# A decoder layer on one core: the loads for splitting the mixer's weights wait for an operand of group 3 of the first feed-forward block, and a split takes five steps of it in place of six

## The chip, the cores and the metric

The kernel runs on one core of one Trainium2 chip. The metric is the device time of one execution in microseconds (us). Five engines work side by side, each on its own list of instructions in a fixed order: PE (TensorE, matrix products), DVE (VectorE), ACT (ScalarE), POOL (GpSimd) and SP (SyncE, which here only issues DMA transfers). ACT also issues DMA transfers, from its own list.

## The reference

One decoder layer over 1024 rows of width 1024, in float32. Cut to what matters here:

```
x <- LN1(alpha*x + 0.5*SwiGLU_1(x))      # first feed-forward block, width 2816
x <- LN2(alpha*x + mixer(x))             # mixer: proj = x @ w_in, sparse attention, gated MLP, @ w_out
x <- LN3(alpha*x + 0.5*SwiGLU_2(x))      # second feed-forward block
```

Products must be exact to almost float32. Each operand is therefore split into a high part and a remainder, and a product is three matmuls (high x high, high x low, low x high).

## The kernel before

**Splitting.** `split` (L84 to L88) makes the two parts of an operand: ACT writes the rounded high part (L87), DVE or POOL subtracts it from the operand (L88).

**The first half of a feed-forward block** (`ffn`, name f1 for the first block) goes over 11 groups, g = 0 to 10. Each group is a Winograd-like scheme of seven products m = 1 to 7; a product is 24 matmuls of 128x512 into a pair of PSUM banks (tile `ab`). Products 1 and 2 of groups 0 to 5 are done ahead, so that the program then goes through five products (6, 7, 5, 4, 3) for groups 1 to 5 and through seven (1, 6, 2, 7, 5, 4, 3) for groups 6 to 10. The weights of group g+1 (four tiles `w`, L342) are loaded while group g is worked on. `left` prepares left operands up to four products ahead: DVE forms sums of weight tiles (L288 to L293), then `parts` splits them; ACT writes `hi`, DVE or POOL writes `lo`. The results of a product are taken out of PSUM by DVE (L382, L413, L416, L423, L429 in the order of the products) and, from group 6 on, after product 1 by an ACT copy (tile `c`, L356). Gated results `h`, `u`, `c` go back to DRAM (`f<-h`, `f<-c`, `f<-u`, L445 to L450), and sums kept in DRAM come back for the next group (`u<-f_c`, `h<-f`, L434, L435).

**The second half** multiplies the stored results by the weights w2 (eleven loads of 1 MB, L504, and `hid` loads, L552; PSUM tiles `y` and `z`).

**Splitting the mixer's weights beside it.** `make_parts` (L99) is a generator that runs through 28 weight pieces: load (L117, SP), split (ACT, DVE, tiles `made`), store the two parts to DRAM (L137, issued by ACT). `product` of the first block takes a step of it after each quarter of a product. The loaded pieces use two buffers (`N_W`), which the `hid` loads use later too; the split pieces use the 15 large buffers, of which 14 hold the split right operand `xs` all through the groups. Each load also has to find its buffer free, so that load i+2 waits for the split of piece i.

**The order.** Outside an early part written in a fixed order, a scheduler places the instructions on each engine by its own model of time and dependencies; an instruction may so stand far ahead of its place in the program. On the chip each engine, and the SP list, goes through its order and waits where an instruction is not ready.

Of the kernel before, what the change touches and what calls it, by code (L numbers as in the profile page):

```python
# [7 lines left out]
F32 = mybir.dt.float32  # L8
# [5 lines left out]
ALU = mybir.AluOpType  # L14
# [17 lines left out]
N_W = PAR["NW"]  # L32
N_BIG = PAR["NB"]
EARLY = 6
class Net:
# [63 lines left out]
    def make_parts(self):  # L99

        nc, ins = self.nc, self.ins
        flat = lambda x: x.rearrange("p k c -> p (k c)")
        todo = [(("A", j), flat(ins["w_inA"][j])) for j in range(4)]
        todo += [(("T", i), flat(ins["w_inT"][i])) for i in (4, 5)]
        todo += [((n, j), flat(ins["w_in" + n][j])) for n in "BC" for j in range(4)]
        todo += [("ws", flat(ins["wsT"]))]
        todo += [(("T", i), flat(ins["w_inT"][i])) for i in range(2)]
        todo += [(("O", i), ins["w_out"][i]) for i in range(4, 8)]
        todo += [(("T", i), flat(ins["w_inT"][i])) for i in range(2, 4)]
        todo += [("wuk", flat(ins["w_ukT"]))]  # L110
        todo += [(("O", i), ins["w_out"][i]) for i in range(4)]
        raws = {}

        def load(i):
            if i < len(todo):
                raws[i] = self.raw("made", (P, todo[i][1].shape[-1]))
                nc.sync.dma_start(raws[i], todo[i][1])  # L117

        load(0)
        for i, (key, src) in enumerate(todo):  # L120
            x, n = raws[i], src.shape[-1]
            load(i + 1)
            if key == "ws":
                y = x.rearrange("p (g c) -> p g c", g=NH)
                nc.gpsimd.affine_select(
                    out=y, in_=y, pattern=[[0, NH], [1, P]], compare_op=ALU.is_ge, fill=0.0, base=0, channel_multiplier=-1
                )
            if key == "wuk":
                nc.scalar.activation(x, x, AF.Copy, scale=0.125)
            yield  # L130
            t = self.large("made", (P, 2, n))
            self.split(x, t[:, 0], t[:, 1])
            yield
            yield
            name = self.name("made")
            self.made[key] = self.dram.tile([P, 2, n], F32, tag=name, name=name)
            nc.scalar.dma_start(self.made[key], t.bitcast(F32))  # L137
            for _ in range(3):
                yield

    def load_w(self, key, s, shape=(P, 1024)):
# [115 lines left out]
    def ffn(self, name, w13, w2, begin, meanwhile, load_acc, norm, after, side=iter(())):  # L257
# [10 lines left out]
        nc, V = self.nc, self.nc.vector  # L268
# [8 lines left out]
        blocks, first_blocks, lefts, xs, sums, due, summed = {}, {}, {}, {}, {}, [], []  # L277

        def left(n):

            for g, m in plan[len(lefts) : n]:
                if g < EARLY and m in (1, 2):
                    lefts[g, m] = self.parts(first_blocks[g, m], V)
                    continue
                a = blocks[g]
                if m == 6:
                    a[5] = self.page("S", (P, 2, HALF))
                    V.tensor_tensor(a[5], a[7], a[4], ALU.add)  # L288
                    a[6] = a[1]
                    V.tensor_tensor(a[7], a[1], a[7], ALU.subtract)  # L290
                    V.tensor_tensor(a[6], a[5], a[1], ALU.subtract)  # L291
                if m == (5 if g else 3):
                    V.tensor_tensor(a[2], a[2], a[6], ALU.subtract)  # L293
                    a[3] = a[2]
                lefts[g, m] = self.parts(a[m], E(PAR["LE"][m - 1] if g > 1 else 0))

        def halves(j):

            if j == 0:
                lefts[0, 1] = tuple(self.page(n, (P, 2, HALF), F32R) for n in ("hi", "lo"))  # L300
            self.split(first_blocks[0, 1][:, j], *(x[:, j] for x in lefts[0, 1]))

        def right(n):

            for i in range(len(xs), min(n, len(xplan))):
                m, k = xplan[i]
                for q in xplan[len(summed) : i + 2 if n > 8 else i + 1]:
                    self.x_sums(*q)
                    summed.append(q)
                if k % 2 == 0:  # L310
                    self.xp = self.large("xs", (P, 2, 2, HALF))
                xs[m, k] = self.xp[:, k % 2, 0], self.xp[:, k % 2, 1]
                self.split(self.x_block(self.X_BLOCK[m])[:, k], *xs[m, k])

        def product(g, m, ps, start=True):
            now = plan.index((g, m))
            for k in range(4):
                if now >= 3:
                    right(8 + (4 * (now - 3) + k + 1) // 2)
                if k == 1:  # L320
                    for f in due:
                        f()
                    due.clear()
                if k or now > 2 * EARLY + 4:
                    left(now + (3 if now < 2 * EARLY + 5 else 1 + (k + PAR["LS"]) // 4))
                w, x = lefts[g, m], xs[m, k]
                for j in range(2):
                    ks = slice(k * P, (k + 1) * P)
                    self.mm3(ps[:, j], (w[0][:, j, ks], w[1][:, j, ks]), x, start and k == 0, k == 3, m in (1, 2, 3, 5))
                if g > 1 and now > 2 * EARLY:  # L330
                    next(side, None)

        def load(g, m, s=slice(0, 2), of=None):
# [18 lines left out]
        def first(g, a):  # L352

            product(g, 1, a)
            c1 = page("c1")
            nc.scalar.activation(c1, a, AF.Copy)  # L356
            return c1

        def first_early(g, a):

            product(g, 1, a)
            c1 = sums[g] = page("c1")

            def keep():
                nc.scalar.activation(c1, a, AF.Copy)
                if g:
                    nc.scalar.dma_start(spill[g], c1)

            due.append(keep)

        def group(g, begun=None):
# [3 lines left out]
            else:  # L375
                a = pair()
                sums[g], h1 = first(g, a), page("h1")
                h11 = h1[:, 0]
            b = pair()
            product(g, 6, b)  # L380
            u2 = sums[g]
            then(lambda b=b: V.tensor_tensor(u2, b, sums[g], ALU.add))  # L382
# [84 lines left out]
        with self.in_order():  # L467
            halves(0)
            right(1)
            halves(1)  # L470
            right(4)
            left(3)
            right(8)
            for g in range(0, EARLY, 2):
                if g == EARLY - 2:
                    for m in (7, 4, 1, 2):
                        load(0, m)
                two = [pair() for _ in range(2)]
                hh = self.raw("hh", (P, 2, HALF))
                for e in range(2):  # L480
                    first_early(g + e, two[e])
                    if g == 0:
                        meanwhile(e)
                for e in range(2):
                    product(g + e, 2, two[e], start=False)

                    def done(g=g + e, h=hh[:, e], ps=two[e]):
                        gated(h, ps)
                        nc.sync.dma_start(hid[g, :, 0], h)
                        if g == 0:  # L490
                            again[g] = None, h

                    due.append(done)
            group(0, again[0])
# [22 lines left out]
        raws, pieces, last, acc = {}, {}, {}, []  # L517
# [50 lines left out]
        for m in order2[:6]:  # L568
# [5 lines left out]
            for k in range(NG):  # L574
# [5 lines left out]
                if m == 7 and k in PAR["NK"]:  # L580
                    t = PAR["NK"].index(k)
# [659 lines left out]
```

## Time and profile before

| | before |
|---|---|
| time, median of 3 runs | 1777.25 us (1776.61 to 1777.44) |
| the profiled execution: its time | 1778.62 us |
| the profiled execution: its span, first to last instruction | 1776.9 us |
| PE busy | 1726.3 us, 97% of the span |
| DVE, ACT, POOL busy | 75%, 45%, 22% |

The first half of the first feed-forward block takes the first 446 us or so of the span, the mixer starts at about 640 us. The profiled execution is 1.37 us above the median.

### The profile page before, as it was taken

To read this page: it belongs to the slowest core of one execution; us is meant where nothing else is said; L and a number is where in the kernel's file an instruction comes from. 1 tells how busy PE (TensorE), PEld (TensorE's weight loads), DVE (VectorE), ACT (ScalarE), POOL (GpSimd) and SP (SyncE) were. 2 spreads that over 40 slices of the span, in tenths; PEclk is the share of its full clock that TensorE was granted. 3 is DMA by queue.
4 is the path that set the end of the run, shared out by engine and by line. 5 is a ranking of instruction groups with operands and counts; after the bars stand their busy time and mean duration, and the time that the engine had idled before them with its cause. 6 is when DMAs were issued, how large, how long until landed. Compare 5 with 4: busy or idle time off the path is not lost.

```text
span 1776.9 us, 22235 instructions
## 1 busy us (share of the span) xinstructions
PE 1726.3 (97%) x8016; PEld 1447.2 (81%) x8016; DVE 1330.1 (75%) x2215; ACT 792.1 (45%) x1346; POOL 396.8 (22%) x287
## 2 busy tenths in 40 slices
PE   8989999999999999999989999999999999999997
PEld 6868778888888888998877888888788888888886
DVE  5779886765895864899979877877777555589586
ACT  5423333423545515667787662452322222355551
POOL 0004242222000361001246321100423222200036
PEclk9999999999999999999999999999999999999999
DMA  7458866757545343225512007335443322754532
GB/s 285 151 222 291 300 252 262 267 203 287 188 123 184 101 163 119 96 87 170 198 36 96 1 1 238 135 119 201 142 178 123 132 89 89 286 192 127 177 101 83
DMA packets 89709, 288.64 MB, mean 162 GB/s; under 512 B 9088, under 2 KB 9600, under 8 KB 85504
## 3 DMA queue, kind: packets, MB, share of 16 engines
q1 hardware_dynamic: 82208, 252.33, 40.2%
q10 hardware_dynamic: 5472, 32.02, 4.5%
q0 software_dynamic: 1920, 2.89, 0.8%
q8 instruction: 63, 1.03, 0.2%
q14 instruction: 46, 0.38, 0.1%
HBM read 195.15 MB, written 89.16 MB: 160 GB/s over the span
## 4 chain that ended last, share of the span: by engine, by line
PE 68%; DVE 8%; ACT 4%; DMA 2%; issue 2%; POOL 1%; SPq 0%; POOLq 0%; ACTq 0%; DVEq 0%
PE ab L152 10%; PE ab L153 10%; PE ab L154 10%; PE y L152 5%; PE y L154 5%; PE y L153 5%; PE z L154 3%; PE z L152 3%; PE z L153 3%; PE pN L152 2%; ACT act L832 2%; PE pN L153 2%; PE pN L154 2%; PE tr L1010 2%; DVE dve L823 1%
## 5 line engine op out<-in xcount | busy, mean ns | idle before, releaser
L152 PE MATMUL ab<-xs,hi 128*128 128x512 f32 x1232 | 482.9, 392 | 23.1 <-DVE c L416 9.2
L153 PE MATMUL ab<-xs,hi 128*128 128x512 f32 x1232 | 481.6, 391 | 0.0
L154 PE MATMUL ab<-xs,lo 128*128 128x512 f32 x1232 | 481.2, 391 | 0.0
L152 PEld LDWEIGHTS ab<-xs,hi 128*128 128x128 f32 x1232 | 232.7, 189 | 76.5 <-issue 17.6
L153 PEld LDWEIGHTS ab<-xs,hi 128*128 128x128 f32 x1232 | 232.7, 189 | 48.5 <-DVE xs L88 0.4
L154 PEld LDWEIGHTS ab<-xs,lo 128*128 128x128 f32 x1232 | 232.7, 189 | 48.4
L88 POOL TENSOR_TENSOR lo<-w,hi 128x1024 fp32r<-128x1024 f32 x54 | 139.8, 2588 | 561.0 <-ACT hi L87 536.7
L87 ACT ACTIVATE hi<-w 128x1024 fp32r<-128x1024 f32 (+1 forms) x134 | 137.6, 1040 | 163.4 <-DVE w L291 123.5
L88 DVE TENSOR_TENSOR lo<-w,hi 128x1024 fp32r<-128x1024 f32 (+1 forms) x80 | 94.8, 1195 | 43.1 <-ACT hi L87 42.5
L88 DVE TENSOR_TENSOR a<-hid,a 128x512 fp32r<-128x512 f32 x132 | 93.5, 708 | 26.1 <-ACT a L87 26.1
L87 ACT ACTIVATE a<-hid 128x512 fp32r<-128x512 f32 x132 | 82.0, 621 | 54.5 <-DMA hid<-f 48.3
L153 PE MATMUL y<-b,a 128*128 128x512 f32 x264 | 102.7, 389 | 0.0
L154 PE MATMUL y<-b,a 128*128 128x512 f32 x264 | 102.7, 389 | 0.0
L153 PE MATMUL z<-b,a 128*128 128x512 f32 x264 | 102.7, 389 | 0.0
L154 PE MATMUL z<-b,a 128*128 128x512 f32 x264 | 102.7, 389 | 0.0
L152 PE MATMUL z<-b,a 128*128 128x512 f32 x264 | 102.5, 389 | 0.0
L152 PE MATMUL y<-b,a 128*128 128x512 f32 x264 | 102.0, 389 | 0.0
L88 DVE TENSOR_TENSOR b<-w,b 128x512 fp32r<-128x512 f32 x110 | 77.2, 702 | 33.0 <-ACT b L87 32.8
L832 ACT ACTIVATE act<-score,tk 128x768 int8<-128x768 f32 (+2 forms) x93 | 87.2, 937 | 29.7 <-DVE tk L844 21.8
L349 ACT ACTIVATE h<-c 128x512 f32<-128x512 f32 x34 | 21.4, 630 | 162.8 <-DVE c L416 115.1
L87 ACT ACTIVATE b<-w 128x512 fp32r<-128x512 f32 x110 | 68.4, 622 | 51.6 <-PE z L154 38.6
L593 POOL TENSOR_TENSOR xacc<-xacc,T 128x512 f32<-128x512 f32 x8 | 13.0, 1652 | 333.8 <-DVE T L566 166.9
(267 smaller groups left out, 3576.9 us busy)
## 6 DMA issues: line engine op xcount, KB each, us to landing
w<-in_ffn_w_dram SPq DMA_DIRECT2D x110, 512.0 KB, 6.5
hid<-f SPq DMA_DIRECT2D x60, 512.0 KB, 3.8
w<-in_ffn_w_dram SPq DMA_DIRECT2D x22, 1024.0 KB, 11.2
f<-h SPq DMA_DIRECT2D x32, 512.0 KB, 3.8
made<-made ACTq DMA_DIRECT2D x16, 1024.0 KB, 6.4
f<-c SPq DMA_DIRECT2D x22, 512.0 KB, 3.9
wo<-made SPq DMA_DIRECT2D x8, 1024.0 KB, 7.6
xr<-x_spill SPq DMA_DIRECT2D x16, 512.0 KB, 5.8
```

The source lines that it names most:

```text
L87: nc.scalar.activation(hi, src, AF.Copy)
L88: (eng or nc.vector).tensor_tensor(lo, src, hi.bitcast(F32), ALU.subtract)
L152: mm(out, a[0], b[0], start=start, stop=False, skip_group_check=skip)
L153: mm(out, a[0], b[1], start=False, stop=False, skip_group_check=skip)
L154: mm(out, a[1], b[0], start=False, stop=stop, skip_group_check=skip)
L349: nc.scalar.activation(t, c[:, 0], AF.Silu)
L593: nc.gpsimd.tensor_tensor(acc[j][:, HALF:], acc[j][:, HALF:], T[j], ALU.add)
L823: V.tensor_scalar(self.marks("dve", s.shape[-1]), s, f, None, ALU.is_lt, ALU.add, accum_out=val[:, j : j + 1])
L832: nc.scalar.activation(out, s, AF.Sign, bias=fj, scale=-1.0, accum_out=val[:, j : j + 1])
L1010: nc.tensor.transpose(pt[:, hh * P : (hh + 1) * P], ps4[hh][:, j * P : (j + 1) * P], self.ident)
```

## The change

The generator starts with group 3 in place of group 2 (`g > 2`), and it takes five steps to a piece in place of six. The first two loads are each preceded by a POOL operation that writes two columns of their buffer, from the newest high part of a left operand (`recent`); a load into that buffer then has to wait for that operation and so for that operand. In the scheduled program this is the high part of product 4 of group 3.

```
         def load(i):
             if i < len(todo):
                 raws[i] = self.raw("made", (P, todo[i][1].shape[-1]))
+                if i < N_W:
+                    t = self.recent.bitcast(F32)[:, 0, :2]
+                    nc.gpsimd.tensor_tensor(raws[i][:, :2], t, t, ALU.subtract)
                 nc.sync.dma_start(raws[i], todo[i][1])
...
             nc.scalar.dma_start(self.made[key], t.bitcast(F32))
-            for _ in range(3):
+            for _ in range(2):
                 yield
...
                 lefts[g, m] = self.parts(a[m], E(PAR["LE"][m - 1] if g > 1 else 0))
+                self.recent = lefts[g, m][0]
...
-                if g > 1 and now > 2 * EARLY:
+                if g > 2 and now > 2 * EARLY:
                     next(side, None)
```

**The list of SP at the weights of group 2.** The names are `made` for a loaded piece, `u_103` and `h_104` for the sums of group 1 that come back, `w_110` to `w_113` for the weights of group 2, `f` for what group 0 stores. Before (the first load of a piece stands one row above):

```order
L117 DMA made_1000<-in_w_inA_dram 128x768
L117 DMA made_1060<-in_w_inA_dram 128x768
L117 DMA made_1121<-in_w_inA_dram 128x768
L434 DMA u_103_783<-f_c_76 128x1024
L435 DMA h_104_784<-f_75 128x512
L445 DMA f_75<-u_88_651 128x512
L342 DMA w_110_834<-in_ffn_w_dram 128x1024
L342 DMA w_111_836<-in_ffn_w_dram 128x1024
L342 DMA w_112_838<-in_ffn_w_dram 128x1024
L449 DMA f_75<-c_89_652 128x1024
L449 DMA f_75<-h_90_653 128x1024
L342 DMA w_113_840<-in_ffn_w_dram 128x1024
```

The same place now:

```order
L346 DMA w_87_649<-in_ffn_w_dram 128x1024
L438 DMA u_103_783<-f_c_76 128x1024
L439 DMA h_104_784<-f_75 128x512
L449 DMA f_75<-u_88_651 128x512
L346 DMA w_110_834<-in_ffn_w_dram 128x1024
L346 DMA w_111_836<-in_ffn_w_dram 128x1024
L346 DMA w_112_838<-in_ffn_w_dram 128x1024
L453 DMA f_75<-c_89_652 128x1024
L453 DMA f_75<-h_90_653 128x1024
L346 DMA w_113_840<-in_ffn_w_dram 128x1024
L454 DMA f_75<-u_88_651 128x512
```

Four loads of pieces are gone from the list ahead of the weights of group 2; the first load of a piece now stands 19 rows behind `w_113`, after the weights of group 4 (`w_162` to `w_165`).

**The list of DVE in group 3.** `S` and `w` with L288 to L293 (now L291 to L296) are sums for the left operands of group 4, `ab` is a PSUM result of group 3, `made` a split. Before:

```order
L382 TENSOR_TENSOR u_165_1186<-ab_1198,u_165_1186 128x1024
L413 TENSOR_TENSOR u_175_1238<-ab_1241,u_165_1186 128x1024
L288 TENSOR_TENSOR S_1279<-w_173_1234,w_174_1236 128x1024
L290 TENSOR_TENSOR w_173_1234<-w_171_1230,w_173_1234 128x1024
L88 TENSOR_TENSOR made_1556<-made_1497,made_1556 128x836
L291 TENSOR_TENSOR w_171_1230<-S_1279,w_171_1230 128x1024
L293 TENSOR_TENSOR w_172_1232<-w_172_1232,w_171_1230 128x1024
L88 TENSOR_TENSOR lo_1284<-w_171_1230,hi_1283 128x1024
L416 TENSOR_TENSOR c_176_1239<-ab_1278,u_175_1238 128x1024
```

Now:

```order
L386 TENSOR_TENSOR u_153_1158<-ab_1170,u_153_1158 128x1024
L88 TENSOR_TENSOR made_1193<-made_1181,made_1193 128x768
L417 TENSOR_TENSOR u_166_1219<-ab_1222,u_153_1158 128x1024
L291 TENSOR_TENSOR S_1258<-w_164_1215,w_165_1217 128x1024
L293 TENSOR_TENSOR w_164_1215<-w_162_1211,w_164_1215 128x1024
L294 TENSOR_TENSOR w_162_1211<-S_1258,w_162_1211 128x1024
L296 TENSOR_TENSOR w_163_1213<-w_163_1213,w_162_1211 128x1024
L88 TENSOR_TENSOR made_1247<-made_1184,made_1247 128x768
L88 TENSOR_TENSOR lo_1263<-w_162_1211,hi_1262 128x1024
L420 TENSOR_TENSOR c_167_1220<-ab_1257,u_166_1219 128x1024
```

The first split of all now stands between the first two results of group 3, the second ahead of the third result. From the first result of a group (L382) to that of the next, DVE had three splits in groups 2 to 4; it now has none in group 2, four in group 3, two in group 4 and four in group 5.

**The list of ACT in group 6.** `c` is the copy of the first result of a group, `hi` a left operand, `h` a gate; the rows run from the copy of group 6 on. Before:

```order
L356 ACTIVATE c_271_1843<-ab_1812 128x1024
L87 ACTIVATE hi_1848<-S_1726 128x1024
L87 ACTIVATE hi_1885<-w_243_1651 128x1024
L87 ACTIVATE made_2037<-made_1974 128x1024
L137 DMA made_2059<-made_2037 128x2048
L349 ACTIVATE h_272_1845<-ab_1812 128x512
L87 ACTIVATE hi_1932<-w_241_1647 128x1024
L87 ACTIVATE made_2103<-made_2029 128x1024
```

Now:

```order
L360 ACTIVATE c_268_1838<-ab_1802 128x1024
L87 ACTIVATE hi_1843<-S_1719 128x1024
L87 ACTIVATE hi_1877<-w_237_1639 128x1024
L87 ACTIVATE made_1669<-made_1607 128x836
L140 DMA made_1690<-made_1669 128x1672
L87 ACTIVATE made_1712<-made_1661 128x836
L353 ACTIVATE h_269_1840<-ab_1802 128x512
L87 ACTIVATE hi_1927<-w_235_1635 128x1024
```

Between the copies of groups 6, 7, 8, 9 and 10 ACT had four, four, three and no splits; it now has five, four, four and five, and one more behind the copy of group 10. Eleven of the 28 splits stood behind the copy of group 6, now nineteen.

## Rows read from the trace of the kernel before

**Rows 1.** The page: the span, and busy time, share and instructions of each engine.

```profile
span 1776.9 us, 22235 instructions
PE 1726.3 (97%) x8016; PEld 1447.2 (81%) x8016; DVE 1330.1 (75%) x2215; ACT 792.1 (45%) x1346; POOL 396.8 (22%) x287
```

**Rows 2.** Stretches of the span: length, then busy time and number of instructions (x) of PE, weight loads, DVE, ACT and POOL, the granted TensorE clock as a share of 2.4 GHz, the DMA share and GB/s.

```profile
90.00:120.00 30.00, 29.08 (x128) 23.47 (x127) 25.24 (x26) 9.93 (x12) 0.00 (x0) 1.00 0.63 232
120.00:150.00 30.00, 24.04 (x98) 19.41 (x97) 23.83 (x18) 8.76 (x10) 10.87 (x4) 0.89 0.73 261
150.00:240.00 90.00, 86.09 (x378) 70.23 (x377) 80.12 (x63) 29.23 (x34) 33.84 (x13) 1.00 0.80 297
240.00:360.00 120.00, 119.38 (x526) 98.22 (x525) 84.33 (x74) 44.21 (x49) 31.27 (x12) 1.00 0.69 261
360.00:390.00 30.00, 30.00 (x134) 24.84 (x133) 19.05 (x19) 11.22 (x13) 10.14 (x4) 1.00 0.63 236
390.00:480.00 90.00, 90.00 (x398) 74.51 (x397) 65.57 (x90) 33.29 (x56) 9.99 (x5) 1.00 0.59 213
480.00:600.00 120.00, 120.00 (x531) 99.37 (x530) 88.61 (x141) 64.03 (x106) 4.87 (x4) 1.00 0.49 156
```

**Rows 3.** The matmuls of PE ahead of which it stood idle, in order of time: start, duration, line and operation, and in brackets the idle time and what ended it.

```profile
104.64 0.47 PE L152 MATMUL ab<-xs,hi 128*128 128x512 f32 x1 [0.72 <-DVE c L406]
133.10 0.77 PE L152 MATMUL ab<-xs,hi 128*128 128x512 f32 x1 [5.96 <-DVE c L416]
179.78 0.47 PE L152 MATMUL ab<-xs,hi 128*128 128x512 f32 x1 [0.96 <-DVE u L382]
...
237.76 0.47 PE L152 MATMUL ab<-xs,hi 128*128 128x512 f32 x1 [2.68 <-DVE u L382]
```

**Rows 4.** DVE, in order of time, around the wait for the weights of group 2.

```profile
111.43 0.68 DVE L442 TENSOR_TENSOR h<-hh,h 128x512 f32<-128x512 f32 x1
...
116.91 1.22 DVE L413 TENSOR_TENSOR u<-ab,u 128x1024 f32<-128x1024 f32 x1
125.68 1.23 DVE L288 TENSOR_TENSOR S<-w,w 128x1024 f32<-128x1024 f32 x1 [7.56 <-DMA w<-in_ffn_w_dram]
...
131.74 1.22 DVE L416 TENSOR_TENSOR c<-ab,u 128x1024 f32<-128x1024 f32 x1
```

**Rows 5.** The SP list, in order of time (start, time from the first to the last issue of the row), and behind it a row of its waits: who waited for whom, us in total, times, the longest.

```profile
82.17 25.02 SPq L117 DMA_DIRECT2D made<-in_w_inA_dram  x4
...
109.20 1.01 SPq L445 DMA_DIRECT2D f<-u  x1
110.25 2.13 SPq L342 DMA_DIRECT2D w<-in_ffn_w_dram  x3
...
113.42 0.33 SPq L449 DMA_DIRECT2D f<-h  x1
113.85 0.36 SPq L342 DMA_DIRECT2D w<-in_ffn_w_dram  x1
...
SPq L117 <- DVE made L88: 119.0, 24, 11.8
```

**Rows 6.** One stretch (columns as in rows 2), and the issues of weight loads up to 480 us: number, KB each, median us from issue to landing.

```profile
118.00:126.00 8.00, 8.00 (x37) 6.64 (x36) 0.44 (x2) 0.00 (x0) 0.00 (x0) 1.00 1.02 415
...
w<-in_ffn_w_dram SPq DMA_DIRECT2D x55, 512.0 KB, 7.2
```

**Rows 7.** ACT, in order of time: the split pieces at the first and the last of twelve in a row, the longest distance between two of them, and the row of its waits for their stores.

```profile
255.33 1.07 ACT L87 ACTIVATE made<-made 128x1024 fp32r<-128x1024 f32 x1 [1.89 <-DMA made<-made]
...
303.80 1.06 ACT L87 ACTIVATE made<-made 128x1024 fp32r<-128x1024 f32 x1 [2.73 <-DMA made<-made]
...
314.73 1.05 ACT L87 ACTIVATE made<-made 128x1024 fp32r<-128x1024 f32 x1
...
361.85 1.06 ACT L87 ACTIVATE made<-made 128x1024 fp32r<-128x1024 f32 x1 [1.02 <-DMA made<-made]
...
ACT made L87 <- DMA made<-made: 65.8, 20, 9.5
```

**Rows 8.** ACT: the copies of groups 6 and 10, the first and the last of five.

```profile
259.82 1.03 ACT L356 ACTIVATE c<-ab 128x1024 f32<-128x1024 f32 x1 [2.87 <-DVE c L440]
...
413.34 1.03 ACT L356 ACTIVATE c<-ab 128x1024 f32<-128x1024 f32 x1 [1.62 <-PE ab L154]
```

**Rows 9.** DVE: a split of a piece while POOL is idle, and one while POOL works.

```profile
155.20 1.02 DVE L88 TENSOR_TENSOR made<-made,made 128x836 fp32r<-128x836 f32 x1
...
221.79 3.15 DVE L88 TENSOR_TENSOR made<-made,made 128x836 fp32r<-128x836 f32 x1 [0.92 <-ACT made L87]
```

**Rows 10.** SP: the loads of the weights w2. ACT: an operand of the second half. A stretch at the end of the groups (columns as in rows 2).

```profile
369.91 0.38 SPq L504 DMA_DIRECT2D w<-in_ffn_w_dram  x1
...
416.19 19.27 SPq L504 DMA_DIRECT2D w<-in_ffn_w_dram  x8
...
447.15 0.63 ACT L87 ACTIVATE a<-hid 128x512 fp32r<-128x512 f32 x1 [2.76 <-DMA hid<-f]
...
430.00:440.00 10.00, 10.00 (x46) 8.29 (x45) 5.03 (x7) 3.58 (x7) 0.00 (x0) 1.00 1.03 410
```

**Rows 11.** POOL: its smallest tensor operations (ns, shortest, median and longest), and its waits up to 480 us.

```profile
L174 POOL TENSOR_TENSOR rstd<-rs,mhalf x26: 542/1192/2739, 603.2 to 1769.7; 128x1 f32<-128x1 f32 x24, 128x4 f32<-128x4 f32 x2
...
POOL lo L88 <- ACT hi L87: 302.8, 19, 131.9
```

More of the change, by code (lines that the diff above doesn't have):

```diff
@@ L116, in load @@
                 raws[i] = self.raw("made", (P, todo[i][1].shape[-1]))
+                if i < N_W:
+                    t = self.recent.bitcast(F32)[:, 0, :2]
+                    nc.gpsimd.tensor_tensor(raws[i][:, :2], t, t, ALU.subtract)
                 nc.sync.dma_start(raws[i], todo[i][1])
@@ L137, in make_parts @@
             nc.scalar.dma_start(self.made[key], t.bitcast(F32))
-            for _ in range(3):
+            for _ in range(2):
                 yield
@@ L295, in left @@
                 lefts[g, m] = self.parts(a[m], E(PAR["LE"][m - 1] if g > 1 else 0))
+                self.recent = lefts[g, m][0]
         def halves(j):
@@ L329, in product @@
                     self.mm3(ps[:, j], (w[0][:, j, ks], w[1][:, j, ks]), x, start and k == 0, k == 3, m in (1, 2, 3, 5))
-                if g > 1 and now > 2 * EARLY:
+                if g > 2 and now > 2 * EARLY:
                     next(side, None)
```

## The prediction

> **What bounds the kernel now.** I read the page first, then stretches of the span, then where PE waits, and then the lists of the engines there. PE is busy for 97% of the span [rows 1], so time can only be won where PE stands idle or runs slowly. The stretches show where that is [rows 2]: 30 us of full work hold 134 matmuls, 90 us hold 398 and 120 us hold 531, which is 120/531 = 0.226 us each. Against this the stretches from 90 us on are short by 134-128 = 6, 134-98 = 36, 398-378 = 20 and 531-526 = 5 matmuls, that is by 1.4, 8.1, 4.5 and 1.1 us, 15.1 us together. This is the span in which pieces of the mixer's weights are split beside the groups. From 360 us to 600 us nothing is lost.
>
> The largest loss has one cause. PE waits 5.96 us, up to 133.10, for the DVE operation L416 that takes a result of group 1 out of PSUM [rows 3]. That operation stands in DVE's list behind sums of group 2's weights, and DVE waits 7.56 us for a weight tile, to 125.68 [rows 4]. The tile is the last of group 2, w_113, issued at 113.85, so that it took 11.8 us to be there [rows 5]. The rest of the 8.1 us is the clock: its mean in that stretch is 0.89 [rows 2], so for about 0.11 x 30 / 0.5 = 6.6 us PE had the lower level, 1.2 GHz in place of 2.4, after the idle time.
>
> **Term 1: the weights of group 2.** Before, four loads of pieces hold the SP list from 82.17 for 25 us [rows 5], because each needs a buffer that an earlier split frees; behind them stand the sums of group 1 (u, h), a store and the weights. Now they are gone from that place. But the next rows of SP show that this isn't the whole wait: the store f<-u, which needs a gate from DVE, is issued only at 109.20, 2.0 us after the pieces' row ends, and w_113 follows f<-h, whose source is ready at 112.1 (L442 [rows 4]). So the load moves only as far as DVE and ACT move. Two splits on DVE fall away ahead of L442, about 1.0 us each [rows 9], and some half a us in which DVE waits for ACT's half of one (an estimate): 2.5 us, so the first issue of this batch comes at about 106.7 and w_113 at about 111. What falls away beside that is traffic. While the tile is awaited, the DMA engines are full, at 415 GB/s [rows 6], and loads and stores of pieces are among what they move. The batch that remains is 256 KB, three tiles, two stores and the last tile of 512 KB each, 3.4 MB, which at 415 GB/s takes 8.2 us: 115 at the earliest; by the median of such loads, 7.2 us [rows 6], w_113 is there at 118. From the sum at 125.68 to the next matmul at 133.10 are 7.4 us [rows 3, 4]; PE ran dry at 127.1, which the loss of 0.7 us at 104.64 [rows 3] no longer delays, so the sum must start by 127.1-0.7-7.4 = 119.0. That is 1 us to spare. I take the 8.1 and the 1.4 us as won and charge 0.5 us for a rest of the wait: -9.0. Bounds: 9.5 won, or, if the tile lands only 2.5 us earlier (123.2), 119.0-123.2 = 4.2 us of waiting stay, and with the clock (8.1 us were lost for 5.96 of waiting) 5.7 us.
>
> The Trainium skill has a rule against my figure here: "DMA: Bandwidth & Descriptors", Bandwidth, says that traffic between HBM and SBUF is held to about 358 GB/s for a core. By it the batch would take 9.5 us, the tile would land 1.3 us later, and the term would be -8.7. The row shows 415 GB/s in this very stretch, so the measurement decides.
>
> **Term 2: groups 2 to 5.** DVE is what is short there: 80.1 of 90 us busy from 150 on, and PE waits for L382, the first result of a group [rows 2, 3]. A split costs DVE 1.0 us, and up to 3.15 us while POOL works [rows 9]. Three splits to each group went with 4.5 us of loss over three group starts, 1.5 each. Now group 2 has none, group 4 two, groups 3 and 5 four. I charge the two heavy groups 1.5 each and the others nothing: 3.0 us in place of 4.5, so -1.5. Bounds: all 4.5 won, or one new wait of the old kind (below).
>
> **Term 3: groups 6 to 10.** A split piece has one large buffer, so ACT can't start the next until the last is stored: it waited 65.8 us for stores in all. From the first to the last of twelve pieces it took 361.85-255.33 = 106.5 us, eleven steps of 9.68 us [rows 7], against a group of (413.34-259.82)/4 = 38.4 us [rows 8]: four pieces, 38.7. So the chain just kept pace with PE, and the loss there was 1.1 us over three groups. Now nineteen pieces stand there, and of five, four, four and five between the copies the last has a second buffer, since the first operands of group 10 free one. That leaves 17 pieces, 16 steps from one to the next, in 4 x 38.4 = 153.5 us, less 3.1 us for the copy and two operands that stand ahead (1.03 us each), plus 4.4 us by which a copy may be late (product 6 lasts 24 x 0.226 = 5.4, the copy 1.03): 154.8 us for 16 x 9.68 = 154.9. Again it just keeps pace, and five of them are shorter (836 columns). I charge the old loss for four and a half groups in place of three, 1.7 in place of 1.1: +0.6. Bounds: -1.1 if it never binds, +20.1 in the third rival.
>
> **Terms at nothing.** The two POOL operations cost 0.5 to 2.7 us each by the smallest of POOL [rows 11]; POOL stands idle for 302.8 us waiting for operands [rows 11], and what they delay is the first load, which the order puts behind the weights of group 4 anyway. If that cover were gone, 2.4 us at the median would be added to the first load. The weights w2 lose the early start of their first load (369.91 [rows 10]): it now waits in SP behind the last pieces, to about 7 us into group 10, and three more follow the very last split. Seven more of the eight late loads took 19 us for buffers that group 10 frees, which doesn't change. The DMA engines, full at 410 GB/s there [rows 10], get some 7 MB more, 17 us of work, while ACT reaches the fifth operand of the second half only at 447 and waits for hid, not w2 [rows 10]. That is 31 us after these loads began (416.19), which leaves room for 7 us in SP's list and a part of the 17, so I add nothing.
>
> **The sum.** -9.0 -1.5 +0.6 = -9.9 us against the profiled execution: 1778.62-9.9 = 1768.7. It lay 1.37 us above the median, so the forecast is **1767.4 us**.
>
> **Rivals.**
> - *All of it goes.* No wait is left: -15.1, 1762.1. For it: half of the DVE-bound stretch has fewer splits. Against: two groups have more. Chance 0.08.
> - *The stall only moves.* In group 3 the second split now stands ahead of the third result. Load, split, store and next split must fit into the four products, 4 x 5.4 = 21.7 us, before PE needs that result out of PSUM: the first load, behind the weights of group 4, lands some 9 us into the group (an estimate: 7.2 us [rows 6] behind an issue 2 us into it), split, store and next split are a step of 9.68, and a remainder and the result, 1.2 us each [rows 4], stand behind: 21.1 us, without any room. If the store meets the weight loads it is later (the longest wait for one was 9.5 [rows 7]), and a wait like that of group 1 with its slow clock comes back: 8.1 us, net -1.8, 1775.5. Chance 0.20.
> - *The chain of splits becomes the bound* (the other side). If a step takes 10.93 us, as from 303.80 to 314.73 [rows 7], 16 take 174.9, 20.1 us more than they have; ACT is then late for the copies and PE waits: -10.5+20.1 = +9.6, 1786.9. It turns to slower than before at (154.8+10.5)/16 = 10.3 us a step; the mean was 9.68. Chance 0.11. The Trainium skill ("TensorE: Matmul & The Clock Gate", on the engines' queues) says that ACT and DVE are strictly first in, first out, so that a waiting split holds all behind it; the 65.8 us of waits agree.
> - *The change does not do what it says.* The last tile of group 2 is late from its own batch, not from the pieces: the 5.7 us of term 1's bound stay, 0.5 of which are charged already: -4.7, 1772.6. Chance 0.08.
> - *The second half starts dry.* If the chain runs 5 us late (10.0 us a step), so do the last weights w2 behind it in SP, and the room above is used up: -4.9, 1772.4. Chance 0.05.
>
> **How the numbers follow.** The forecast has 0.48. A measurement of this kernel tells about 0.2%, 3.5 us, from no change, so faster means below 1773.7 and slower above 1780.8. Faster: the forecast, the first, the fourth and the fifth case, and a little of the second, 0.72; same: most of the second and a mild third, 0.17; slower 0.11. The range goes from the first rival's 1762.0 to 1775.5, where the second ends; beyond lie half of the second and the third.
>
> **What would show it.** Right: no load of a piece on SP before about 160 us; DVE's wait for w in group 2 under 2 us; 120 to 150 us with 130 or more matmuls and a clock of 1.00; the copy of group 10 about 10 us earlier than 413.34; splits of pieces until after it, ACT's waits for stores near 65 us, and 1 to 3 us of waits for DVE in groups 3 and 5. Wrong: an idle time over 4 us with a lower clock in groups 3 to 5, a distance of over 10.3 us between pieces behind group 6, or waits for w2 or hid at the start of the second half.

## The result and the profile after

The change makes the kernel slower: 1786.82 us median of 6 runs (1784.37 to 1791.16) against 1777.98 us for the kernel before, ratio 1.0055 with a 95% interval from 1.0044 to 1.0066. The forecast was 1767.4 us, with a range that ended at 1775.5. The profiled execution of after has a span of 1782.6 us (before: 1776.9 [rows 1]).

The stretches of after, with the columns of rows 2:

```profile
90.00:120.00 30.00, 30.00 (x134) 24.83 (x133) 21.79 (x22) 6.76 (x8) 0.00 (x0) 1.00 0.39 131
120.00:150.00 30.00, 27.63 (x122) 22.58 (x121) 26.30 (x21) 7.45 (x9) 10.12 (x4) 1.00 0.41 150
150.00:240.00 90.00, 89.26 (x393) 73.44 (x392) 72.59 (x63) 29.36 (x36) 31.68 (x14) 1.00 0.71 260
240.00:360.00 120.00, 116.62 (x511) 95.30 (x511) 89.81 (x75) 44.15 (x50) 33.33 (x13) 1.00 0.68 257
360.00:390.00 30.00, 29.48 (x131) 24.11 (x130) 18.06 (x16) 11.84 (x14) 10.45 (x4) 1.00 0.66 263
390.00:480.00 90.00, 81.58 (x347) 66.73 (x348) 65.26 (x86) 31.64 (x49) 10.46 (x4) 0.94 0.78 297
480.00:600.00 120.00, 118.07 (x521) 97.44 (x521) 86.12 (x139) 68.44 (x114) 0.00 (x0) 1.00 0.50 156
```

Up to 240 us nearly all of the old loss is gone: 12 and 5 matmuls are missing where 6+36 and 20 were [rows 2]. But 20 are missing from 240 to 360 us (5 before), 51 from 390 to 480 us (none before), with a mean clock of 0.94, and 10 from 480 to 600 us (none before). The matmuls of PE ahead of which it stood idle say where:

```profile
127.69 0.47 PE L155 MATMUL ab<-xs,hi 128*128 128x512 f32 x1 [2.37 <-DVE c L420]
199.56 0.47 PE L155 MATMUL ab<-xs,hi 128*128 128x512 f32 x1 [0.74 <-DVE u L386]
265.88 0.50 PE L155 MATMUL ab<-xs,hi 128*128 128x512 f32 x1 [0.75 <-DVE h L354]
299.81 0.50 PE L155 MATMUL ab<-xs,hi 128*128 128x512 f32 x1 [0.99 <-DVE c L386]
329.24 0.47 PE L155 MATMUL ab<-xs,hi 128*128 128x512 f32 x1 [1.61 <-DVE c L433]
...
458.67 1.65 PE L155 MATMUL y<-b,a 128*128 128x512 f32 x3 [7.43 <-ACT b L87]
482.35 0.50 PE L155 MATMUL y<-b,a 128*128 128x512 f32 x1 [1.93 <-ACT T L591]
```

The wait of 5.96 us at group 2 [rows 3] has become one of 2.37, and a new one of 7.43 us stands at the start of the second half. The places in the program that can be found in both traces give the account:

| us from the start | before | after | difference | change since the place above |
|---|---|---|---|---|
| copy of group 6 (ACT) | 259.82 | 249.35 | -10.5 | -10.5 |
| first matmul of `y` (PE) | 445.8 | 440.2 | -5.6 | +4.9 |
| first result of `y` out of PSUM (ACT, `T`) | 474.39 | 481.72 | +7.3 | +12.9 |
| end of the span | 1776.9 | 1782.6 | +5.7 | -1.6 |

(The copies: after at 249.35 and 410.06, before [rows 8].) So the change wins 10.5 us in groups 1 to 5, gives 4.9 back in groups 6 to 10 and 12.9 at the start of the second half. The last 1.6 us were not followed to a place. What ACT and SP do there, after:

```profile
408.48 0.33 SPq L120 DMA_DIRECT2D made<-in_w_out_dram  x1
409.62 0.38 SPq L556 DMA_DIRECT2D hid<-f  x1
...
413.52 1.56 SPq L508 DMA_DIRECT2D w<-in_ffn_w_dram  x1
...
419.84 20.28 SPq L508 DMA_DIRECT2D w<-in_ffn_w_dram  x9
440.21 4.83 SPq L556 DMA_DIRECT2D hid<-f  x2
...
457.47 0.63 ACT L87 ACTIVATE a<-hid 128x512 fp32r<-128x512 f32 x1 [13.86 <-DMA hid<-f]
```

In before the fifth operand from `hid` was split at 447.15 [rows 10], though its load was issued only 0.6 us earlier (439.60). After, the load is issued at 440.21, and ACT stands idle for 13.86 us until the tile is there, 17.3 us behind its issue. All eleven w2 loads are issued after 413 us (before, one at 369.91 and ten from 410.61 on), and two tiles of `hid`, which before were loaded from 355 us on, come behind the last piece too. One stretch, after and then before:

```profile
410.00:460.00 50.00, 42.57 (x185) 34.95 (x185) 26.52 (x39) 14.24 (x22) 7.76 (x3) 0.94 1.02 405
```

```profile
410.00:460.00 50.00, 50.00 (x222) 41.42 (x221) 31.61 (x47) 18.68 (x31) 7.15 (x3) 1.00 0.77 284
```

For 50 us the DMA engines are never free, at 405 GB/s; before they moved 284. The difference, 121 GB/s times 50 us, is 6 MB. Most of it is the first w2 tile (1 MB), two tiles of `hid` (1 MB) and the last pieces (a load of 0.5 MB, three stores of 1 MB): 5.5 MB.

### The profile page after: what moved, and what is told of

Read it like the earlier page. It is cut to its first block, busy times and chain, and to the rows that moved or that the text cites. A ratio compares the mean times of both kernels' runs of the same rounds, so it can differ in the third digit from the quotient of the medians.

```text
span 1782.6 us, 22237 instructions
## 1 busy us (share of the span) xinstructions
PE 1724.5 (97%) x8016; PEld 1444.9 (81%) x8016; DVE 1332.0 (75%) x2215; ACT 793.2 (44%) x1346; POOL 396.3 (22%) x289
## 4 chain that ended last, share of the span: by engine, by line
PE 68%; DVE 12%; DMA 12%; ACT 5%; issue 2%; POOL 1%; SPq 0%; ACTq 0%; POOLq 0%; DVEq 0%
PE ab L155 10%; PE ab L157 10%; PE ab L156 10%; DMA made<-made 6%; PE y L155 5%; PE y L157 5%; PE y L156 5%; DMA w<-in_ffn_w_dram 3%; PE z L157 3%; PE z L155 3%; PE z L156 3%; PE pN L155 2%; PE pN L156 2%; PE pN L157 2%; PE tr L1014 2%
## 5 line engine op out<-in xcount | busy, mean ns | idle before, releaser
L597 POOL TENSOR_TENSOR xacc<-xacc,T 128x512 f32<-128x512 f32 x8 | 12.4, 1585 | 346.1 <-DVE T L570 346.1
```

The costliest lines, as they stand in the source:

```text
L597: nc.gpsimd.tensor_tensor(acc[j][:, HALF:], acc[j][:, HALF:], T[j], ALU.add)
```

## The experiments

Two theories stood against each other. **Backlog**: the pieces end so late that 5.5 MB more fall into a stretch in which w2 already fills the DMA engines, and `hid` lands late. **Engines**: ACT and DVE, kept at splits up to 414 us in place of 362, are late with the operands.

**1. Which part acts.** The scheduled program of "five steps and group 3" without the wait is that of the kernel before on every engine; with the wait, five steps and six give the same program too. So the change is the wait, and the group only sets which operand is waited for.

```
-                if i < N_W:
-                    t = self.recent.bitcast(F32)[:, 0, :2]
-                    nc.gpsimd.tensor_tensor(raws[i][:, :2], t, t, ALU.subtract)
```

> The change without the wait: five steps to a split and the start at group 3, but no POOL operation ahead of the first two loads. The lists of all five engines are those of the kernel before, instruction by instruction, so every theory expects 1777.9 us and a ratio to the kernel before of 1.000 (0.999 to 1.001), with the last split of a piece near 362 us and no wait of PE at the start of the second half. If it is over 0.2% away, the change acts through something that the lists don't show.

Measured: 1776.98 us, ratio 0.9997 (0.9987 to 1.0007), last split at 360.7 us. As expected.

**2. The wait alone**, for an operand of the group before (six steps, `g > 1`).

> The wait alone: six steps to a split, and the pieces begin beside group 2, so that the load waits for a left operand of the group before, some 30 us earlier than in the changed kernel (about 132 us in place of 162). Backlog theory (the chain of splits ends so late that its last loads and stores, the first w2 tile and two tiles of hid fall into the 40 us in which the w2 tiles already fill the DMA engines, and the third tile of hid lands late): the last split comes 15 to 28 us earlier than 414 us, the wait of PE at the start of the second half shrinks from 7.4 us to 2 to 4 us, time about 1781 us (1778 to 1784). Engines theory (ACT and DVE, still busy with splits in group 10, are late with operands of the second half): the wait goes wholly once no split stands in group 10; with one or two left it stays above 5 us, time 1784 to 1787.

Measured: 1776.23 us, ratio 0.9995 (0.9985 to 1.0006): no change. The pieces run from 146.4 to 404.6 us (after: 169.2 to 414.4), PE has no idle time at the start of `y`, and 1.73 us at 473.88. Ten us earlier are enough to take the large wait away. Both theories allow it, but the last split comes later than the backlog theory said (386 to 399 us), and the time is better than either said. Its copies are at 253.04 and 410.65 us: it wins less than the change up to group 6 (6.8 us) and gives 4.1 of that back on the way to group 10.

**3. Without the last four pieces.** Their loads, splits and stores are left out; four pieces of the same weight that were split earlier take their place, so that part of the computation is left out.

```
-        todo += [(("O", i), ins["w_out"][i]) for i in range(4)]
...
+            if key[0] == "O":
+                self.made["O", key[1] - 4] = self.made[key]
```

> The changed kernel without the loads, splits and stores of the last four pieces (their place is taken by the four pieces of the same weight that were split earlier, so that part of the computation is left out). The last split should come near 378 us in place of 414 us, as before the change nearly (362). Backlog theory: the first w2 tile and two tiles of hid are loaded before 400 us, the third tile of hid lands within 8 us, no wait of PE above 2 us at the start of the second half: 12.4 us less there, and up to 2 us less in groups 9 and 10, 1773 to 1775 us. Engines theory: the same direction, since the splits in group 10 are gone too; this run tells whether the late chain is the cause at all. If the wait of 7 us stays, both are wrong.

Measured: 1769.34 us, ratio 0.9957 (0.9940 to 0.9973), faster than the 1773 to 1775 expected, last split at 388.0 us (378 expected), first result of `y` at 469.1 us. The stretch that lost most, of this kernel and then of after:

```profile
446.00:475.00 29.00, 29.00 (x130) 24.01 (x129) 27.83 (x47) 14.15 (x28) 0.00 (x0) 1.00 0.57 185
```

```profile
446.00:475.00 29.00, 21.57 (x85) 17.31 (x84) 18.84 (x33) 9.14 (x17) 0.00 (x0) 0.82 0.72 265
```

The late end of the chain is the cause, and without it (and without the work of these four pieces) the change does nearly what the forecast said. Which of the two theories it is this run can't tell. The rows can: in after ACT has 9 and DVE 19 of 29 us busy there, less than without the wait. They stand idle for DMA, not late from work.

**4. The order of the loads.** The last four w2 tiles are held back until the third tile of `hid` is there.

```
-        for k in range(NG):
+        for k in range(7 if name == "f1" else NG):
             load2(k)
...
                     raws[m] = r
+                    if m == 1 and k == 4 and name == "f1":
+                        for i in range(7, NG):
+                            W[i] = self.large("w2", (P, 2, 2, HALF), F32)
+                            nc.gpsimd.tensor_tensor(W[i][:, 0, 0, :2], r[:, 0, :2], r[:, 0, :2], ALU.subtract)
+                            nc.sync.dma_start(W[i], ...)
```

> The changed kernel with one difference in the first FFN: the last four w2 tiles (4 MB) are loaded only once the third tile of hid is there (a POOL operation on each of them reads that tile). Pieces, splits and their times stay as in the changed kernel. Backlog theory: the third tile of hid then no longer stands behind 9 MB of w2, is there 5 to 8 us after its issue in place of 17, PE's wait of 7.4 us falls to under 2 us, and with the slow clock some 9 to 12 us are won: 1776 us (1773 to 1779). Engines theory: nothing changes at ACT and DVE, the wait stays, 1785 to 1789.

Measured: 1785.55 us, ratio 1.0049 (1.0033 to 1.0065): a miss for the backlog theory as I had put it. ACT, and PE, in the profiled execution, which at 1792.90 us is the slowest of the five:

```profile
448.28 0.63 ACT L87 ACTIVATE a<-hid 128x512 fp32r<-128x512 f32 x1 [2.95 <-DMA hid<-f]
...
458.81 0.63 ACT L87 ACTIVATE b<-w 128x512 fp32r<-128x512 f32 x1 [6.77 <-DMA w<-in_ffn_w_dram]
469.63 0.63 ACT L87 ACTIVATE a<-hid 128x512 fp32r<-128x512 f32 x1 [10.19 <-DMA hid<-f]
```

```profile
470.83 2.07 PE L155 MATMUL y<-b,a 128*128 128x512 f32 x4 [7.00 <-ACT b L87]
484.82 0.79 PE L155 MATMUL y<-b,a 128*128 128x512 f32 x1 [4.16 <-ACT T L596]
```

The tile comes 9.2 us earlier (448.28) and PE doesn't wait for it. But now the held tiles are late, and a later tile of `hid` behind them: the wait of 7 us moves from 458.67 to 470.83. So it was not this one queue position alone: with either of these two orders some tile comes late. The Trainium skill ("DMA: Bandwidth & Descriptors", Queues, rings and completion order) says that each DMA engine takes up the work of one issuer in the order in which it was issued; the load that waited 17.3 us behind nine w2 loads, and the waits that moved with the order, agree.

**5. The bytes alone.** The kernel before, with eleven more stores of 0.5 MB and nothing at ACT, DVE or POOL, once behind group 9 and once behind group 7.

```
+                if g == 9 and name == "f1":
+                    for i in range(11):
+                        nc.sync.dma_start(spare[i], h2)
```

> The kernel before, with nothing added at ACT, DVE or POOL: behind group 9 the result h2 of that group is stored eleven times more to spare rows (5.5 MB), about 414 us, which is what the late chain of the changed kernel brought into this stretch. Backlog theory: the DMA engines, at 368 GB/s from 420 to 450 us in the kernel before, can't take 13.4 us more of work at 410 GB/s; the third tile of hid lands 8 to 13 us later than in the kernel before and PE waits 4 to 10 us at the start of the second half: 1777 + 6 to 14 us, 1783 to 1791, with no split of a piece behind 362 us. Engines theory: no difference beyond 2 us, 1776 to 1779.

> The same eleven stores, behind group 7 (about 338 us), where the DMA engines move some 270 GB/s and w2 isn't awaited. Backlog theory: they delay one store of a piece and the loads of one group by up to 13 us, which costs at most 3 us of PE, and nothing at the start of the second half: 1777 to 1780 us. If it costs as much as the late stores, the place doesn't matter, and 5.5 MB anywhere in groups 6 to 10 cost 10 us.

Measured, late: 1789.32 us, ratio 1.0073 (1.0056 to 1.0089), with the last split at 362.8 us as before. ACT waits for `hid` and PE for ACT, as after the change:

```profile
461.20 0.63 ACT L87 ACTIVATE a<-hid 128x512 fp32r<-128x512 f32 x1 [10.96 <-DMA hid<-f]
```

```profile
462.40 1.42 PE L152 MATMUL y<-b,a 128*128 128x512 f32 x4 [4.47 <-ACT b L87]
485.99 0.50 PE L152 MATMUL y<-b,a 128*128 128x512 f32 x1 [2.64 <-ACT T L591]
```

That settles it: 5.5 MB in this stretch make the wait, without a single split there. The engines theory falls. One thing differs from the change: these stores stand in SP's own list, so that eight w2 loads are issued 15 us later too (from 431.29 on, before 416.19), and the third tile of `hid` 4 us later (443.61).

Measured, early: 1787.72 us, ratio 1.0065 (1.0047 to 1.0083). This was expected at 1777 to 1780, and it was wrong. The second half starts without a wait, but PE waits within group 8:

```profile
372.21 0.77 PE L152 MATMUL ab<-xs,hi 128*128 128x512 f32 x1 [5.61 <-DVE c L417]
```

The four weight loads of the next group are issued only at 359.29 us, 12.1 us later than before, and this is the stall of group 2 [rows 3] at another place, again with a slow clock behind it (a mean of 0.83 from 360 to 380 us). The 270 GB/s of the expectation fit a mean over 30 us (271 from 335 to 365 us). Where the block falls, the kernel before had little room already:

```profile
338.00:360.00 22.00, 22.00 (x99) 18.20 (x98) 13.40 (x12) 7.65 (x8) 7.60 (x3) 1.00 0.92 348
```

**6. A faster chain.** A piece is split and stored in two halves, each with half of the one large buffer; then the same from group 2 on.

```
+        big = self.large("made", (P, 2, 2, 512))
...
+            for h in range(2):
+                t, c = big[:, h, :, : n // 2], slice(h * n // 2, (h + 1) * n // 2)
+                self.split(x[:, c], t[:, 0], t[:, 1])
+                yield
+                nc.scalar.dma_start(self.made[key][:, :, c], t.bitcast(F32))
+                yield
```

> The changed kernel, with each piece split and stored in two halves, each of them with one half of the single large buffer, so that one half is split while the other is stored. Same loads, same bytes; ACT and DVE get 56 operations of half the size in place of 28. Backlog theory: a piece takes about 7 us in place of 9.1, the last split comes 25 to 45 us earlier than 414 us, the first w2 tile and two tiles of hid are loaded before 400 us, and the 12.9 us at the start of the second half are won: 1774 us; of the 4.9 us lost in groups 7 to 10 up to 3 come back too, since ACT waits less for stores: 1770 to 1775. Engines theory: some 0.2 us more of ACT and of DVE for each piece make groups 7 to 10 worse, 1780 to 1790.

> As the run with halves, but the pieces begin beside group 2, so that the first load waits for a left operand some 30 us earlier. Backlog theory: the last split comes at 345 to 360 us, nothing is lost at the start of the second half; groups 2 and 3 have three or four splits more and lose 1 to 4 us (the run with the wait alone had its copy of group 6 3.7 us later than the changed kernel): 1770 to 1776 us, level with or a little behind the run with halves. If groups 7 to 10 then lose nothing, it is the faster one, 1768 us.

Measured: 1779.00 us, ratio 1.0018 (1.0009 to 1.0027), and 1779.65 us, 1.0019 (1.0009 to 1.0029). The wait before `y` is gone, as expected. The last split comes at 395.9 and 379.3 us, later than forecast (369 to 389 and 345 to 360). And the run with halves loses where after did not:

```profile
150.00:240.00 90.00, 83.18 (x362) 67.08 (x361) 73.31 (x67) 28.79 (x42) 31.74 (x14) 1.00 0.79 279
```

36 matmuls are missing, 8.1 us. PE waits there 6.8 us for results that DVE takes out of PSUM (after: 0.74), and DVE waits 7.8 us for ACT's part of the half pieces (after: 4.0). So the denser chain costs groups 3 to 5 some 7 us more than in after, and the first matmul of `y` comes at 450.8 us (after: 440.2): most of what the end had won. That DVE's waits are the cause is read from these rows and not tested. Both runs were forecast too fast, as the price of the chain at DVE was left out there as in term 3 (below).

**7. The last pieces later.** The last four, then eight, pieces are loaded into pages and split beside products of the second half. All parts are computed.

```
+                raws[i] = (self.raw if i < 24 else self.page)("made", ...)
...
+            if i == 24:
+                while not self.second:
+                    yield
+                load(i)
...
+                if m in (2, 6):
+                    self.second = True
+                    next(side, None)
```

> The changed kernel, with the last four pieces split later: they are loaded into pages and split beside the products m=2 and m=6 of the second half of the first FFN, after w2 has been loaded. Backlog theory: up to the copy of group 10 and over the start of the second half this is the run without these pieces (its copies at 251.1 and 408.2 us, no wait at the start of y, 1769.3 us); four splits, about 1.1 us of ACT and of DVE each, and 6 MB come back beside products of the second half, where DVE is busy 57 of 90 us and the DMA engines move 150 GB/s or less: 0 to 3 us, 1769 to 1773 us, faster than both kernels. If a wait comes back there (hid or an operand late behind the pieces), 1774 to 1779.

> As the run with four pieces later, but eight (in the products m=2, 6, 5 and 3). The last split in the first half then comes near 350 us. If each split in groups 8 and 9 costs PE something (after the change 41.65 us from the copy of group 9 to that of group 10 with five splits, 38.4 with two), another 1 to 3 us are won against the run with four: 1767 to 1771 us. If the groups with four splits lose nothing and the second half pays for them, 1771 to 1776.

Measured: 1768.23 us, ratio **0.9958** (0.9946 to 0.9970), and 1767.54 us, 0.9955 (0.9942 to 0.9969). Both are faster than both kernels, as the backlog theory said, and level with each other. With four later, the stretch of experiment 3 has `29.00 (x129)`; with eight later also the end of the groups is full:

```profile
330.00:420.00 90.00, 90.00 (x399) 74.55 (x398) 52.38 (x49) 26.92 (x31) 27.32 (x11) 1.00 0.58 216
```

**8. The same without the wait**, to see what the wait is worth.

> The kernel before, without any part of the change, with its last four pieces split in the second half of the first FFN as in the run with four pieces later. If that run's 8 us come from the wait (the stall of group 2, 9.5 us of PE, is gone, and only the late end had taken the gain back), this kernel keeps that stall and has nothing to win behind it, since in the kernel before the last split comes at 362 us, long before w2: 1775 to 1777 us, within 0.1% of the kernel before. If moving the four pieces is itself worth 8 us, 1767 to 1770.

Measured: 1774.71 us, ratio 0.9984 (0.9973 to 0.9994). Moving four pieces is worth 0.16% by itself, a little more than expected; the wait is worth the rest, 0.9958/0.9984, 0.26% or 4.6 us (some 2 to 7 by the intervals). That is about what after had in hand at the first matmul of `y` (5.6 us), not the 9.9 of the forecast.

**9. Whose time the splits take in groups 6 to 10.** Eight pieces later, with POOL in place of DVE for the remainder of the other twenty.

```
-            self.split(x, t[:, 0], t[:, 1])
+            self.split(x, t[:, 0], t[:, 1], nc.gpsimd if i < 20 else None)
```

> As the run with eight pieces later, but in the first half the second half of a split (the subtraction) is made by POOL in place of DVE. It takes some 2.6 us there in place of 1.2 us, so a piece takes about 10.7 us in place of 9.1, and the last split comes 25 to 35 us later than in the run with eight, still ahead of group 10. If the loss of groups 3 to 9 is DVE's (PE waits for results that DVE takes out of PSUM), groups 7 and 8 go from 39.5 and 41.9 us to near 38.3, and 3 to 5 us are won: 1764 to 1768. If it is ACT's (a split that waits for a store, with the copy and the gates behind it) nothing changes: 1768 to 1773. If POOL slows DVE down while it works, it is slower than the run with eight.

Measured: 1777.28 us, ratio 0.9999 (0.9985 to 1.0013), over a wide spread (1769.67 to 1780.31), where 1764 to 1768 or 1768 to 1773 was expected. The stretches of the profiled execution, which is the fastest of the ten:

```profile
150.00:240.00 90.00, 85.44 (x375) 69.86 (x374) 67.17 (x52) 28.27 (x33) 45.92 (x21) 1.00 0.70 255
...
240.00:330.00 90.00, 90.00 (x398) 74.55 (x398) 59.31 (x50) 33.39 (x40) 42.38 (x19) 1.00 0.62 231
```

From 240 to 330 us, where the run with eight pieces later misses 17 matmuls, nothing is missing, which speaks for DVE as the way by which the loss came. But 23 are missing from 150 to 240 us, where that run had 396 of 398, so that the groups pass at other times, and 11 from 330 to 420 us, where it was full. As a version it wins nothing, and why its times spread stays open.

## Why the prediction was wrong

**The step that failed is a term at nothing: w2.** The prediction saw the 7 MB, put them at 17 us of DMA work, and set them against "room": 31 us from the first of the eight loads to the fifth operand of the second half. That is room in SP's list. The DMA engines had none of it, and the prediction itself quoted them as full, at 410 GB/s [rows 10]. The row of before up to the moment at which the third tile of `hid` was there, and the one of the stretch behind it:

```profile
410.00:447.00 37.00, 37.00 (x165) 30.65 (x164) 18.61 (x26) 10.53 (x16) 7.15 (x3) 1.00 0.93 344
446.00:475.00 29.00, 29.00 (x129) 24.02 (x128) 29.00 (x49) 14.21 (x27) 0.00 (x0) 1.00 0.49 163
```

So most of what was added came out as delay. 5.5 MB at 405 GB/s are 13.6 us; the third tile of `hid`, last in the list, came 10.3 us later (457.47 in place of 447.15), as the engines had a little room before it was due (busy for 0.93). ACT had waited for this tile by 2.76 us already [rows 10], so there was nothing in hand. Measured, +12.9 us in place of 0. On PE, from the first matmul of `y` to the first of `z` (445.8 to 505.6 us before, 440.2 to 512.4 after), it is 12.4 us: 7.43 and 1.93 us of idle time, and 3.0 from the clock, which stood partly at the lower of its two levels behind the idle time (a mean of 0.82 from 446 to 475 us). That 13.6 and 12.9 lie so close is in part luck, since they are not the same quantity. PE and DVE were busy for all 29 us of the second row before the change, which left nothing to make it up with.

**Terms 1 and 2 held as a sum:** -10.5 us at the copy of group 6, as forecast, but by luck, as two errors of 2 us cancel. Singly, the stretch of term 1 still misses 12 matmuls of the 42, so it won 6.8 us and not 9.0. The issue of the last weight tile came at 110.63, as estimated (111), but DVE could use it at 120.24, not 118; even without the pieces' traffic the tile took 9.6 us from its issue (before: 11.8), against the median of 7.2 [rows 6]. Term 2 won more, 15 matmuls, 3.4 us in place of 1.5. The rival in which the stall moves to group 3 did not come: from 150 to 240 us the largest wait is 0.74 us.

**Term 3 was mis-sized:** +4.9 us in place of +0.6. Where the splits stand was right (five, four, four, five and one), and the chain did not fall behind: the 16 steps from the first to the last but one of the pieces between the copies are 9.33 us each, against 9.68 assumed:

```profile
254.41 0.91 ACT L87 ACTIVATE made<-made 128x836 fp32r<-128x836 f32 x1 [2.15 <-DMA made<-made]
...
403.64 2.01 ACT L87 ACTIVATE made<-made 128x1024 fp32r<-128x1024 f32 x2 [1.37 <-DMA made<-made]
```

So ACT's copies were not the price. DVE was: PE stood idle for 4.9 of the 180 us from 240 to 420 us (before: 0.6), and each of these waits in after ended with an operation of DVE. DVE's own waits from 240 to 420 us, after and then before (who waits for whom, us, times, longest):

```profile
DVE made L88 <- ACT made L87: 38.8, 14, 6.2
```

```profile
DVE made L88 <- ACT made L87: 10.9, 6, 5.0
```

A split whose ACT half waits for the store holds DVE as well, and results of products stand behind it in DVE's list. In group 7:

```profile
308.60 1.23 DVE L88 TENSOR_TENSOR made<-made,made 128x1024 fp32r<-128x1024 f32 x1 [5.90 <-ACT made L87]
...
318.10 1.23 DVE L88 TENSOR_TENSOR made<-made,made 128x1024 fp32r<-128x1024 f32 x1 [1.77 <-ACT made L87]
...
327.88 1.21 DVE L433 TENSOR_TENSOR c<-ab,c 128x1024 f32<-128x1024 f32 x1
```

These 7.7 us of waiting stand ahead of the result at 327.88, for which PE waits 1.61 us at 329.24. They are not the whole of it: the wait of 0.99 us at 299.81 stands behind three operations of DVE of 2.9 us each (290.13 to 298.55) while POOL works; two of them took 0.7 us in the other groups. The prediction quoted the rule that a waiting split holds all behind it, and priced it for ACT alone. Experiment 9, which takes DVE out of the splits, clears the stretch from 240 to 330 us in the execution that was profiled; how the 4.9 us divide between DVE's waits and its longer operations is not shown.

**The rivals.** The last one named the right place, the start of the second half, but had w2 late there and not `hid`, made it depend on a chain 5 us late and priced it at 5 us. The fourth was right in part: behind its own batch alone the last tile of group 2 was still late, and 12 matmuls, 2.7 us, stay lost where it priced 5.7. The third one's time (1786.9) is the measured one by accident: its condition, over 10.3 us a step, was not met (9.33), and its price was put on ACT's copies. The two POOL operations are nothing, as said (0.19 us each).

**The signs named beforehand.** Right: the first load of a piece at 162.3 us, a clock of 1.00 from 120 to 150 us, the last split behind the copy of group 10; ACT's waits for stores were somewhat longer (75.3 us, 65 expected). Wrong: 122 matmuls from 120 to 150 us (130 expected), DVE's wait for w in group 2 (4.55 us, under 2 expected), the copy of group 10 (3.3 us earlier, not 10), and the wait for `hid`, which the prediction had listed as what would make it wrong.

## What to carry to other kernels

Work that is put off still has its bytes: when a side job is moved, look up what the DMA engines are doing where it now ends, and where they are at their full rate price the added bytes as delay of the last tile that is due, not against free time in a list. Here bytes over rate gave 13.6 us and the tile came 10.3 us later. When a job moves later for the sake of its start, move its end too: here the change alone lost 0.55%, and with the last four pieces put behind the w2 loads it won 0.42%. A split in two halves on two engines held both lists when the first half waited: DVE stood 38.8 us for ACT's halves.

## What the runs showed that I had not expected

5.5 MB of stores in a stretch with a mean of 270 GB/s cost nearly as much (10.9 us) as in the one that is nearly full (12.5 us): the mean of 30 us hid 22 us at 348 GB/s, just where the block fell and ahead of one group's weights. Room is looked up in the very microseconds in which the bytes will move, up to the next load that is due. And DMA engines that were busy at 284 GB/s on average over 50 us took 405 GB/s over the same 50 us, without a gap, only by way of a load that came 17.3 us behind its issue.
